# The first SwiGLU block of a decoder trunk: two products advanced together, and the last squares of the final norm summed in PSUM

## The chip, the cores and the metric

The kernel is one program on one core of a Trainium2 chip. The metric is the device time of one execution in microseconds; three executions of the kernel before took 2440.54, 2441.75 and 2447.37 us, median 2441.75 us.

## What the kernel computes

A decoder trunk of two layers over 512 tokens of width 1024, in fp32. Each layer adds four sublayers to the residual stream, each on an RMS-normed input: a SwiGLU feed-forward block (weight 1/2), a token mixer (short convolution, a gated recurrence and an RWKV-7 group side by side), cross-attention into 256 memory tokens, and a second feed-forward block. A final RMSNorm ends it. The parts that the change touches are the first feed-forward block and the two ends of the norm:

```
def rmsnorm(x, g):
    xf = xf * lax.rsqrt(jnp.mean(xf * xf, axis=-1, keepdims=True) + EPS)
    return (xf * g)
def swiglu_ffn(x, w_in, w_out):
    gate, up = jnp.split(x @ w_in, 2, axis=-1)       # 2 x 2816 columns
    return (jax.nn.silu(gate) * up) @ w_out
h = x
for l in range(2):
    h = h + 0.5 * swiglu_ffn(rmsnorm(h, ffn1_norm[l]), ffn1_w_in[l], ffn1_w_out[l])
    ...
return rmsnorm(h, final_norm)
```

## The kernel before

The stream is held transposed: `h[0]` to `h[7]`, each 128 of the 1024 channels by 512 tokens. Every large product runs in a split form: an operand is a high part (rounded to fp32r by ScalarE) and a low part (the rest, by VectorE), and `mm3` issues three matmuls: high x high, high weight x low input, low weight x high input. One product of a 128-column weight block with the eight chunks is 24 matmuls of 128x512 into one PSUM bank. The factor of the norm is not applied to the input: the gain of the norm is folded into the split of `h[d]`, and the product is multiplied by the reciprocal root afterwards (`gated`, with `n.rstd`).

A feed-forward block goes through 22 pairs of weight blocks (f = 0 to 21, in three slabs of 8, 7 and 7): a gate product, an up product, then `gated` on VectorE and ScalarE, which frees the two banks. After each slab eight output products add to `h`. Below, W0 and U0 are the gate and up weights of f = 0, G1 and U1 those of f = 1, G2 the gate weights of f = 2.

`load_w` brings one weight block: a copy issued by SP into a staging buffer (`wst`, two of them), the high part on ScalarE (`whi`, three) and the low part on VectorE (`wlo`, three). `Weights` keeps the planned sequence; `take` hands out the next block and calls `ahead(2)`, and `group` calls `ahead(3)` after a product, so loads are asked for two or three blocks ahead. PSUM's eight banks are three `pb` (`big`), three `pm` (`small`) and two `pt` (`serial`, otherwise used by the mixer).

The order on TensorE is the order of the program. ScalarE and VectorE get an order from a clock model in the kernel: each instruction is given a modelled start, and `issue_in_order` chains the instructions of each of the two engines by it. The order on SP is left to the framework, which lets copies go ahead of where the program asks for them: the four copies of `memT`, asked for at f = 9, are issued at 15.35 us. The mixing stages are also interleaved by a planner (`Fill.run`) that reads the same clock model.

The beginning: `start` loads W0 in four pieces of 256 columns, and behind the copy of each piece it issues two chunks of x and their splits; then come the eight squares (`Norm.chunk`, ScalarE) and seven adds (VectorE) whose column sums give the first norm. `ffn` then runs the gate product of f = 0 into `pb`, the up product (its weights U0 loaded whole), loads the constants `cst`, runs the gate product of f = 1, asks for the sums (`n.begin`: `rms_sums`, 4 fp32 matmuls against ones, then VectorE, GpSimd, VectorE), runs the up product of f = 1 into a `pm` bank, and only then spreads the factor over the partitions (`rms_spread`, 8 small matmuls) for `gated`. The gate product of f = 2 takes the `pb` bank that `gated` of f = 0 frees.

The end: as each of the last eight output products is added to `h[d]`, `chunk(d)` squares it, adds the square to `acc` and scales a copy by the gain. After the last one `rms_sums`, `rms_spread`, eight multiplications and eight copies out follow.

Lines: in the trace all instructions of VectorE, ScalarE and SP carry line 285 and those of TensorE line 340, the two recording helpers, so the tiles tell them apart: `s` is any 128x512 slot, `xT` the input, `pb`, `pm`, `pt` the banks.

Of the kernel before, what the change touches and what calls it, by code (L numbers as in the profile page):

```python
# [11 lines left out]
F32R = mybir.dt.float32r  # L12
I32 = mybir.dt.int32
AF = mybir.ActivationFunctionType
ALU = mybir.AluOpType
# [3 lines left out]
P = 128  # L19
# [310 lines left out]
def trunk(ctx: ExitStack, tc: tile.TileContext, a, out, parts=("ffn1", "mix", "xa", "ffn2"), dbg=None):  # L330
# [38 lines left out]
    def f32(x):  # L369
        return x.bitcast(F32)  # L370
# [53 lines left out]
    def col(l, name, i=0):  # L424
        o = l * VL + VOFF[name] + i
        return vec[:, o:o + 1]
# [31 lines left out]
        ve.tensor_scalar(omka[:, l * 3:l * 3 + 3], vec[:, o:o + 3], -1.0, 1.0, ALU.mult, ALU.add)  # L458


    def load_w(src, cols, piece=1024, between=None):
        st, hi, lo = wst.get(), whi.get(F32R), wlo.get(F32R)
        for o in range(0, cols, piece):
            cs = slice(o, min(cols, o + piece))
            sp.dma_start(st[:, cs], src[:, cs])
            if between:
                between(o // piece)
            se.activation(hi[:, cs], st[:, cs], AF.Copy)
            ve.tensor_tensor(lo[:, cs], st[:, cs], f32(hi[:, cs]), op=ALU.subtract)
        return hi, lo  # L470

    class Weights:
# [138 lines left out]
            ve.scalar_tensor_tensor(lo, src, scale, f32(hi), op0=ALU.mult, op1=ALU.subtract)  # L611
        return hi, lo

    def rms_sums(acc, n):

        k = n // P
        ps = small()
        for i in range(k):
            te.matmul(ps[:, i:i + 1], acc[:, i * P:(i + 1) * P], ones[:, 0:1], start=True, stop=True)
        r = clock.tile(tiny, [P, 4], F32, "rms", 4)  # L620
        ve.tensor_scalar(r[:, :k], ps[:, :k], 1.0 / D, EPS, ALU.mult, ALU.add)
        gp.tensor_tensor(r[:, :k], r[:, :k], mhalf.to_broadcast([P, k]), op=ALU.pow)
        rh = clock.tile(tiny, [P, 4], F32R, "rmsh", 4)
        rl = clock.tile(tiny, [P, 4], F32R, "rmsl", 4)
        ve.tensor_copy(rh[:, :k], r[:, :k])
        ve.tensor_tensor(rl[:, :k], r[:, :k], f32(rh[:, :k]), op=ALU.subtract)
        return rh, rl
# [11 lines left out]
    class Norm:  # L639
        def __init__(self, l, name):  # L640
            self.l, self.name = l, name
            self.acc = self.r = self.sums = self.waiting = None
            self.x = []
            self.scaled = []

        def chunk(self, d):
            if self.acc is None:
                self.acc = sl.get()
                se.activation(self.acc, h[d], AF.Square)
            else:  # L650
                sq = sl.get()
                se.activation(sq, h[d], AF.Square)
                ve.tensor_tensor(self.acc, self.acc, sq, op=ALU.add)
                sl.put(sq)
            if self.name is not None:
                self.x.append(split(h[d], col(self.l, self.name, d)))
            elif self.l is None:
                y = sl.get()
                se.activation(y, h[d], AF.Copy, scale=vec[:, L * VL + d:L * VL + d + 1])
                self.scaled.append(y)  # L660

        def begin(self):
            if self.sums is None:
                self.sums = rms_sums(self.acc, T)
                sl.put(self.acc)

        @property
# [21 lines left out]
                sl.put(*x)  # L689
            sl.put(self.r)  # L690

    def start(name, src):

        n = Norm(0, name)

        def load(i):
            for d in (2 * i, 2 * i + 1):
                sp.dma_start(h[d], a["xT"][:, d, :])
                n.x.append(split(h[d], col(0, name, d)))

        W.plan[0][2] = load_w(src, 1024, 256, load)
        n.name = None
        for d in range(ND):
            n.chunk(d)
        return n


    def ffn(l, which, n, nxt, between=None):
# [13 lines left out]
        for f0, f1 in SLABS:  # L722
            act = []
            for f in range(f0, f1):
                if f in between:
                    between[f]()
                pg = big()
                group(pg, w_in[l, f], 1024, n.x)
                if f or "w" not in between:
                    n.begin()  # L730
                pu = small() if first else big()
                group(pu, w_in[l, NF + f], 1024, n.x)
                if f == 0 and "w" in between:
                    first = pg, pu
                    sp.dma_start(cst, a["cst"])
                    ve.tensor_copy(identr, ident)
                    continue
                if first:
                    gated(*first)
                    first = None  # L740
                gated(pg, pu)
            last = f1 == NF
            if last:
                n.release()
            for d in range(ND):
                po = big()
                k = f1 - f0
                group(po, w_out[l, d, :, f0 * P:f1 * P], k * P, act)
                ve.scalar_tensor_tensor(h[d], po, 0.5, h[d], op0=ALU.mult, op1=ALU.add)
                if last:  # L750
                    nxt.chunk(d)
            for x in act:
                sl.put(*x)
# [866 lines left out]
    plans = {"ffn1": lambda l: plan_ffn(l, 1), "mix": plan_mix, "xa": plan_xa, "ffn2": lambda l: plan_ffn(l, 2)}  # L1620
    for l, s in steps:
        plans[s](l)
    n = start("ffn1_norm", a["ffn1_w_in"][0, 0])
    for i, (l, s) in enumerate(steps):
        nxt = Norm(steps[i + 1][0], norms[steps[i + 1][1]]) if i + 1 < len(steps) else Norm(None, None)
        if s == "ffn1":
# [75 lines left out]
```

## Time and profile before

| | us |
|---|---|
| median of three executions | 2441.75 |
| the profiled execution | 2447.83 |
| its span, first to last instruction | 2446.0 |
| TensorE busy in the span | 2398.0 |
| VectorE busy | 1389.6 |
| ScalarE busy | 995.7 |
| first matmul | 7.66 |
| last large matmul ends | 2429.55 |

Times in the rows are counted from the start of the span. A timeline row gives start, length, engine, line, operation, output <- inputs, and how many instructions are merged in it; in brackets stands the engine's idle time before it and what ended that. Consecutive matmuls overlap in the record, so the pace is read from start to start.

### The profile page before, as it was taken

The page shows a single profiled execution, that of the slowest core. Times are in us where ns is not written, and L with a number is a line of the kernel's source. Part 1 is how long each engine was busy: PE and PEld are TensorE (multiplying, and loading weights), DVE is VectorE, ACT ScalarE, POOL GpSimd, SP SyncE. Part 2 cuts the span into 40 slices and gives each one's busy share as a digit, 9 for nine tenths or more (in the row PEclk, how much of TensorE's full clock was granted, in tenths as well). Part 3 has the DMA queues.
Part 4 walks back from the last instruction along what each step waited for, and adds up shares of the span by engine and source line. Part 5 has one row for each costly group of instructions (what it writes and reads, how often), then busy time and mean ns, then how long its engine had stood idle before and what let it go on. Part 6 is the DMA issues. An engine that isn't in the chain of part 4 may idle for free. (4 is left out here: it accounts for less than half of the span.)

```text
span 2446.0 us, 33922 instructions
## 1 busy us (share of the span) xinstructions
PE 2398.0 (98%) x13812; PEld 1971.5 (81%) x13812; DVE 1389.6 (57%) x2172; ACT 995.7 (41%) x1416; POOL 20.8 (1%) x22
## 2 busy tenths in 40 slices
PE   7999999999999999999999999999999999999997
PEld 6888887787878888888888888877887788888886
DVE  5444456798866654444544444567987756434444
ACT  4222235756654432222332222466475534323222
POOL 0000000000000000000000000000000000000000
PEclk9999999999999999999999999999999999999998
DMA  5333333243422233333323333423333313232332
GB/s 166 95 95 94 99 109 103 82 150 122 134 84 80 65 103 97 102 93 97 95 95 100 98 95 95 132 82 121 121 117 118 96 48 100 92 98 94 96 99 74
DMA packets 94315, 246.84 MB, mean 101 GB/s; under 512 B 22096, under 2 KB 24784, under 8 KB 94160
## 3 DMA queue, kind: packets, MB, share of 16 engines
q1 hardware_dynamic: 90848, 238.56, 31.6%
q10 hardware_dynamic: 3312, 6.12, 0.7%
q8 instruction: 109, 1.79, 0.3%
q14 instruction: 46, 0.38, 0.1%
HBM read 230.48 MB, written 14.16 MB: 100 GB/s over the span
## 5 line engine op out<-in xcount | busy, mean ns | idle before, releaser
L340 PE MATMUL pb<-s,whi 128*128 128x512 f32 (+1 forms) x6160 | 1897.6, 390 | 24.3 <-ACT whi L285 16.7
L340 PEld LDWEIGHTS pb<-s,whi 128*128 128x128 f32 x6160 | 1150.2, 189 | 268.1 <-ACT whi L285 20.6
L340 PE MATMUL pb<-s,wlo 128*128 128x512 f32 (+1 forms) x3080 | 1193.5, 388 | 5.6 <-DVE wlo L285 5.6
L285 ACT ACTIVATE whi<-wst 128x1024 fp32r<-128x1024 f32 (+5 forms) x445 | 434.2, 976 | 1033.9 <-PE pb L340 637.6
L340 PEld LDWEIGHTS pb<-s,wlo 128*128 128x128 f32 x3080 | 582.9, 189 | 123.9 <-DVE wlo L285 7.7
L285 DVE TENSOR_TENSOR wlo<-wst,whi 128x1024 fp32r<-128x1024 f32 (+5 forms) x445 | 498.4, 1121 | 134.8 <-ACT whi L285 127.1
L285 DVE TENSOR_TENSOR s<-pb,s 128x512 f32<-128x512 f32 (+1 forms) x345 | 236.0, 689 | 465.0 <-PE pb L340 443.4
L285 ACT ACTIVATE s<-s 128x512 f32<-128x512 f32 (+2 forms) x458 | 282.7, 626 | 246.8 <-DVE s L285 241.2
L285 DVE TENSOR_TENSOR s<-s,s 128x512 f32<-128x512 f32 (+3 forms) x526 | 317.0, 621 | 97.0 <-ACT s L285 92.1
L285 DVE SCALAR_TENSOR_TENSOR s<-pb,s 128x512 f32<-128x512 f32 x96 | 66.4, 692 | 234.5 <-PE pb L340 234.5
L285 ACT ACT_TABLE_LOAD x74 | 94.9, 1283 | 2.9 <-PEq L1690 1.7
L285 DVE SCALAR_TENSOR_TENSOR s<-s,vec,s 128x512 fp32r<-128x512 f32 (+2 forms) x100 | 74.3, 748 | 3.8 <-ACT s L285 2.9
L340 PEld LDWEIGHTS pm<-s,s 64*64 64x64 f32 (+2 forms) x1104 | 60.4, 158 | 10.0 <-issue 4.3
L340 PE MATMUL pm<-s,s 64*64 64x64 f32 (+2 forms) x1104 | 66.7, 248 | 1.7 <-DVE s L285 0.9
L285 ACT ACTIVATE s<-s,vec 128x512 fp32r<-128x512 f32 (+1 forms) x90 | 64.3, 718 | 3.3 <-DMA s<-xT 1.7
L340 PE MATMUL pb<-whi,s 128*128 128x512 f32 x128 | 49.5, 427 | 3.3 <-DVE s L285 3.3
L340 PEld LDWEIGHTS pm<-s 64*64 64x64 f32 (+1 forms) x1152 | 33.8, 132 | 4.7 <-issue 3.2
L340 PE MATMUL pm<-s 64*64 64x32 f32 (+1 forms) x1152 | 36.3, 216 | 0.0
L285 POOL TENSOR_TENSOR rms<-rms,mhalf 128x4 f32<-128x4 f32 (+1 forms) x10 | 17.1, 1714 | 2120.7 <-DVE rms L285 2120.7
L340 PEld LDWEIGHTS pb<-whi,s 128*128 128x128 f32 x128 | 24.1, 188 | 10.8 <-DVE s L285 4.1
L285 DVE TENSOR_TENSOR s<-s 128x256 f32<-128x256 f32 (+1 forms) x79 | 31.7, 439 | 0.2
L285 ACT ACTIVATE s<-pb 128x512 fp32r<-128x512 f32 x32 | 19.0, 594 | 29.5 <-PE pb L340 29.2
(106 smaller groups left out, 741.1 us busy)
## 6 DMA issues: line engine op xcount, KB each, us to landing
wst<-ffn_w_in SPq DMA_DIRECT2D x175, 512.0 KB, 3.4
wst<-w_mix_in SPq DMA_DIRECT2D x58, 512.0 KB, 3.6
wst<-ffn_w_out SPq DMA_DIRECT2D x64, 448.0 KB, 3.3
wst<-ffn_w_out SPq DMA_DIRECT2D x32, 512.0 KB, 3.5
wst<-xattn_wk SPq DMA_DIRECT2D x16, 512.0 KB, 4.4
wst<-xattn_wv SPq DMA_DIRECT2D x16, 512.0 KB, 3.7
wst<-xattn_wq SPq DMA_DIRECT2D x16, 512.0 KB, 3.5
wst<-xattn_wo SPq DMA_DIRECT2D x32, 256.0 KB, 2.6
```

What stands on the lines that cost most here:

```text
L285: ins = fn(*args, **kw)
L340: self.pin(nc.tensor.matmul(*args, **kw))
```

## The change

`start` now takes the sources of both W0 and U0, and issues for each quarter a piece of W0, a piece of U0 and two chunks of x; the splits follow in the order piece of W0, chunk, piece of U0, chunk. Behind the last chunk it issues the copy of `cst`, `W.ahead(3)` (the load of G1) and the copy of the identity, all ahead of the squares. For f = 0 of the first block `ffn` takes both weights, and advances the two products in turns, three matmuls each per chunk; the banks are one `pb` and one `pt`. The second `take` asks for U1's load before the 48 matmuls. The up product of f = 1 goes to the other `pt`. The call of `n.begin` that asks for the sums stands behind the gate product of f = 1, where it stood. In the final norm the square of the last chunk isn't added to `acc`: `rms_sums` issues four matmuls on `acc` and four more, accumulating, on the last square.

```diff
--- before.py
+++ after.py
@@ -458,15 +458,12 @@
         ve.tensor_scalar(omka[:, l * 3:l * 3 + 3], vec[:, o:o + 3], -1.0, 1.0, ALU.mult, ALU.add)
 
 
-    def load_w(src, cols, piece=1024, between=None):
+    def load_w(src, cols):
         st, hi, lo = wst.get(), whi.get(F32R), wlo.get(F32R)
-        for o in range(0, cols, piece):
-            cs = slice(o, min(cols, o + piece))
-            sp.dma_start(st[:, cs], src[:, cs])
-            if between:
-                between(o // piece)
-            se.activation(hi[:, cs], st[:, cs], AF.Copy)
-            ve.tensor_tensor(lo[:, cs], st[:, cs], f32(hi[:, cs]), op=ALU.subtract)
+        cs = slice(0, cols)
+        sp.dma_start(st[:, cs], src[:, cs])
+        se.activation(hi[:, cs], st[:, cs], AF.Copy)
+        ve.tensor_tensor(lo[:, cs], st[:, cs], f32(hi[:, cs]), op=ALU.subtract)
         return hi, lo
 
     class Weights:
@@ -611,12 +608,16 @@
             ve.scalar_tensor_tensor(lo, src, scale, f32(hi), op0=ALU.mult, op1=ALU.subtract)
         return hi, lo
 
-    def rms_sums(acc, n):
+    def rms_sums(acc, n, last=None):
 
         k = n // P
         ps = small()
         for i in range(k):
-            te.matmul(ps[:, i:i + 1], acc[:, i * P:(i + 1) * P], ones[:, 0:1], start=True, stop=True)
+            te.matmul(ps[:, i:i + 1], acc[:, i * P:(i + 1) * P], ones[:, 0:1], start=last is None or i == 0,
+                      stop=last is None, skip_group_check=last is not None)
+        for i in range(k if last is not None else 0):
+            te.matmul(ps[:, i:i + 1], last[:, i * P:(i + 1) * P], ones[:, 0:1], start=False, stop=True,
+                      skip_group_check=True)
         r = clock.tile(tiny, [P, 4], F32, "rms", 4)
         ve.tensor_scalar(r[:, :k], ps[:, :k], 1.0 / D, EPS, ALU.mult, ALU.add)
         gp.tensor_tensor(r[:, :k], r[:, :k], mhalf.to_broadcast([P, k]), op=ALU.pow)
@@ -639,12 +640,15 @@
     class Norm:
         def __init__(self, l, name):
             self.l, self.name = l, name
-            self.acc = self.r = self.sums = self.waiting = None
+            self.acc = self.last = self.r = self.sums = self.waiting = None
             self.x = []
             self.scaled = []
 
         def chunk(self, d):
-            if self.acc is None:
+            if d == ND - 1 and self.name is None and self.l is None:
+                self.last = sl.get()
+                se.activation(self.last, h[d], AF.Square)
+            elif self.acc is None:
                 self.acc = sl.get()
                 se.activation(self.acc, h[d], AF.Square)
             else:
@@ -661,7 +665,7 @@
 
         def begin(self):
             if self.sums is None:
-                self.sums = rms_sums(self.acc, T)
+                self.sums = rms_sums(self.acc, T, self.last)
                 sl.put(self.acc)
 
         @property
@@ -689,16 +693,28 @@
                 sl.put(*x)
             sl.put(self.r)
 
-    def start(name, src):
+    def start(name, srcs):
 
         n = Norm(0, name)
-
-        def load(i):
+        ws = [(wst.get(), whi.get(F32R), wlo.get(F32R)) for _ in srcs]
+        for i in range(4):
+            cs = slice(256 * i, 256 * i + 256)
+            for (st, hi, lo), src in zip(ws, srcs):
+                sp.dma_start(st[:, cs], src[:, cs])
             for d in (2 * i, 2 * i + 1):
                 sp.dma_start(h[d], a["xT"][:, d, :])
+        for i in range(4):
+            cs = slice(256 * i, 256 * i + 256)
+            for u, (st, hi, lo) in enumerate(ws):
+                se.activation(hi[:, cs], st[:, cs], AF.Copy)
+                ve.tensor_tensor(lo[:, cs], st[:, cs], f32(hi[:, cs]), op=ALU.subtract)
+                d = 2 * i + u
                 n.x.append(split(h[d], col(0, name, d)))
-
-        W.plan[0][2] = load_w(src, 1024, 256, load)
+        for e, w in zip(W.plan, ws):
+            e[2] = w[1:]
+        sp.dma_start(cst, a["cst"])
+        W.ahead(3)
+        ve.tensor_copy(identr, ident)
         n.name = None
         for d in range(ND):
             n.chunk(d)
@@ -724,17 +740,20 @@
             for f in range(f0, f1):
                 if f in between:
                     between[f]()
+                if f == 0 and "w" in between:
+                    first = big(), serial()
+                    two = [group_steps(ps, W.take(w_in[l, i], 1024), n.x) for ps, i in zip(first, (0, NF))]
+                    for _ in zip(*two):
+                        pass
+                    for g in two:
+                        next(g, None)
+                    W.ahead(AHEAD)
+                    continue
                 pg = big()
                 group(pg, w_in[l, f], 1024, n.x)
-                if f or "w" not in between:
-                    n.begin()
-                pu = small() if first else big()
+                n.begin()
+                pu = serial() if first else big()
                 group(pu, w_in[l, NF + f], 1024, n.x)
-                if f == 0 and "w" in between:
-                    first = pg, pu
-                    sp.dma_start(cst, a["cst"])
-                    ve.tensor_copy(identr, ident)
-                    continue
                 if first:
                     gated(*first)
                     first = None
@@ -1620,7 +1639,7 @@
     plans = {"ffn1": lambda l: plan_ffn(l, 1), "mix": plan_mix, "xa": plan_xa, "ffn2": lambda l: plan_ffn(l, 2)}
     for l, s in steps:
         plans[s](l)
-    n = start("ffn1_norm", a["ffn1_w_in"][0, 0])
+    n = start("ffn1_norm", (a["ffn1_w_in"][0, 0], a["ffn1_w_in"][0, NF]))
     for i, (l, s) in enumerate(steps):
         nxt = Norm(steps[i + 1][0], norms[steps[i + 1][1]]) if i + 1 < len(steps) else Norm(None, None)
         if s == "ffn1":
```

## Rows read from the trace of the kernel before

**Rows 1.** The page: busy time by engine, and TensorE's granted clock in 40 slices of the span.
```profile
PE 2398.0 (98%) x13812; PEld 1971.5 (81%) x13812; DVE 1389.6 (57%) x2172; ACT 995.7 (41%) x1416; POOL 20.8 (1%) x22
...
PEclk9999999999999999999999999999999999999998
```
**Rows 2.** Busy time in stretches of the span: stretch, length, busy us (instructions) of TensorE, its weight loads, VectorE, ScalarE, GpSimd; mean granted clock; DMA share; GB/s.
```profile
15.51:20.49 4.98, 0.74 (x4) 0.30 (x3) 4.57 (x7) 3.31 (x5) 0.00 (x0) 0.85 0.84 290
...
33.55:42.89 9.34, 7.40 (x42) 6.27 (x40) 3.52 (x7) 3.97 (x5) 1.93 (x1) 1.00 0.20 58
42.89:46.40 3.51, 3.51 (x8) 2.81 (x9) 3.42 (x6) 2.39 (x4) 0.00 (x0) 0.51 0.51 149
46.40:2429.55 2383.15, 2362.08 (x13677) 1942.52 (x13675) 1357.12 (x2105) 970.95 (x1380) 17.68 (x16) 0.99 0.32 99
2429.55:2446.00 16.45, 3.36 (x16) 3.12 (x16) 6.79 (x13) 1.83 (x3) 1.01 (x1) 0.58 0.34 128
```
**Rows 3.** Timeline of TensorE, first 47 us.
```profile
7.66 1.22 PE L340 MATMUL pb<-s,whi 128*128 128x512 f32 x2 [7.66 <-ACT whi L285]
...
12.38 0.40 PE L340 MATMUL pb<-s,wlo 128*128 128x512 f32 x1
...
15.13 0.39 PE L340 MATMUL pb<-s,wlo 128*128 128x512 f32 x1
17.92 0.73 PE L340 MATMUL pb<-s,whi 128*128 128x512 f32 x2 [2.40 <-ACT whi L285]
20.49 0.80 PE L340 MATMUL pb<-s,wlo 128*128 128x512 f32 x1 [1.84 <-DVE wlo L285]
...
25.78 0.43 PE L340 MATMUL pb<-s,wlo 128*128 128x512 f32 x1
...
33.55 0.95 PE L340 MATMUL pm<-cst,s 128*128 128x1 f32 x8
...
39.94 0.22 PE L340 MATMUL pm<-identr,rmsh 128*128 128x128 f32 x1
...
42.89 1.22 PE L340 MATMUL pb<-s,whi 128*128 128x512 f32 x2 [1.94 <-DVE s L285]
...
46.40 0.39 PE L340 MATMUL pb<-s,wlo 128*128 128x512 f32 x1
```
**Rows 4.** Timeline of ScalarE, first 19 us.
```profile
5.29 0.72 ACT L285 ACTIVATE s<-s,vec 128x512 fp32r<-128x512 f32 x1 [1.17 <-DMA s<-xT]
...
7.21 0.40 ACT L285 ACTIVATE whi<-wst 128x256 fp32r<-128x256 f32 x1
...
11.07 1.38 ACT L285 ACTIVATE s<-s,vec 128x512 fp32r<-128x512 f32 x2
...
12.66 4.26 ACT L285 ACTIVATE s<-s 128x512 f32<-128x512 f32 x8
16.82 1.99 ACT L285 ACTIVATE whi<-wst 128x1024 fp32r<-128x1024 f32 x2
```
**Rows 5.** Timeline of VectorE, 5 to 22 us.
```profile
6.04 0.75 DVE L285 SCALAR_TENSOR_TENSOR s<-s,vec,s 128x512 fp32r<-128x512 f32 x1 [0.44 <-ACT s L285]
...
13.83 5.47 DVE L285 TENSOR_TENSOR s<-s,s 128x512 f32<-128x512 f32 x7 [0.25 <-ACT s L285]
19.22 2.35 DVE L285 TENSOR_TENSOR wlo<-wst,whi 128x1024 fp32r<-128x1024 f32 x2
```
**Rows 6.** The copies: a stretch of 2 us (columns as in rows 2), two kinds of copy of the first 24 us with count, KB each and median us from issue to landing, and two issues on SP.
```profile
8.00:10.00 2.00, 2.00 (x6) 1.41 (x6) 2.00 (x5) 2.00 (x4) 0.00 (x0) 1.00 1.04 385
...
s<-xT SPq DMA_DIRECT2D x8, 256.0 KB, 4.8
...
cst<-cst SPq DMA_DIRECT2D x1, 736.0 KB, 6.5
...
13.61 0.33 SPq L285 DMA_DIRECT2D wst<-ffn_w_in  x1
15.35 2.71 SPq L285 DMA_DIRECT2D s<-memT  x4
```
**Rows 7.** Timeline of VectorE in the steady part of the block: the first read of each product's bank, for two products in a row.
```profile
50.25 0.69 DVE L285 TENSOR_TENSOR s<-pb,s 128x512 f32<-128x512 f32 x1 [3.04 <-PE pb L340]
...
55.69 0.69 DVE L285 TENSOR_TENSOR s<-pb,s 128x512 f32<-128x512 f32 x1 [3.30 <-PE pb L340]
```
**Rows 8.** Timeline of the end.
```profile
2429.16 0.39 PE L340 MATMUL pb<-s,wlo 128*128 128x512 f32 x1
2429.58 0.69 DVE L285 SCALAR_TENSOR_TENSOR s<-pb,s 128x512 f32<-128x512 f32 x1 [2.67 <-PE pb L340]
2430.31 0.63 ACT L285 ACTIVATE s<-s 128x512 f32<-128x512 f32 x1 [3.51 <-DVE s L285]
...
2430.97 0.69 DVE L285 TENSOR_TENSOR s<-s,s 128x512 f32<-128x512 f32 x1 [0.69 <-ACT s L285]
...
2431.72 1.42 PE L340 MATMUL pm<-cst,s 128*128 128x1 f32 x8 [2.17 <-DVE s L285]
2433.18 0.16 DVE L285 TENSOR_SCALAR rms<-pm 128x4 f32<-128x4 f32 x1 [1.51 <-PE pm L340]
```
**Rows 9.** Who waited for whom on TensorE from 45 to 2429 us.
```profile
PE pb L340 <- DVE s L285: 7.9, 6, 2.2
```

## Prediction

> **What bounds the kernel now.** The page comes first: TensorE is busy in 98% of the span, and its granted clock is below full in the last slice alone [rows 1]. So only idle time of TensorE, or time at the lower of its two clocks (1.2 in place of 2.4 GHz), can be won. The stretches then say where that is: from 46.40 to 2429.55 us TensorE idles 2383.15 - 2362.08 = 21.1 us in all; the rest lies in the first 46 us and in the tail [rows 2]. The change touches just these two. So the timeline of TensorE is read there. It starts at 7.66, and stands still three times: 2.40 us before 17.92 (for `whi` of U0), 1.84 before 20.49 (for `wlo` of U0), 1.94 before 42.89 (for a bank that VectorE reads) [rows 3]. The timelines of ScalarE and VectorE show why: ScalarE runs eight squares from 12.66 before the weights at 16.82, VectorE seven adds from 13.83 before `wlo` at 19.22 [rows 4, 5]. At the end every step waits for the last.
>
> The warm pace: a product's 24 matmuls take 55.69 - 50.25 = 5.44 us, 0.227 each [rows 7]. At the lower clock a start comes every 0.43 us: 11 of them from 7.66 to 12.38, 8 from 42.89 to 46.40, 12 from 20.49 to 25.78 [rows 3]; the granted clock of the second of these stretches is 0.51 [rows 2]. So a stall of 1.9 us costs some 1.7 us more behind it.
>
> **The beginning.** Removed are the waits for U0 and for the third `pb` bank; added are three more SP issues, and U0 in four small conversions in place of one large.
>
> First matmul. W0's and U0's first pieces are ahead of chunk 0, so it comes behind 128 KB more. At the 385 GB/s of [rows 6] that is 0.34 us; the queue is not yet at that rate then, so I take 0.6: 5.29 becomes 5.9 [rows 4]. The piece of W0 is now converted ahead of it, not at 7.21 behind chunk 1. With 0.72 us of ScalarE the first matmul is at 6.65; the second needs the low part, 0.75 us of VectorE [rows 4, 5], and starts at 7.4. From both sides: 1.0 us earlier than 7.66, or 0.6 later, if both pieces are converted first.
>
> The 48 matmuls. If the clock rises where it did, about 12.38, then 1 + (12.38 - 7.4) / 0.427 = 12.7 matmuls are out by then. The other 35.3 take 8.0 us at the warm pace: both products end at 20.4. Is x there in time? ScalarE began chunks 6 and 7 at 11.07 and needed both by 11.8 [rows 4]; U0's 512 KB go ahead of the last of them now, 1.36 us at 385 GB/s, so it lands by 13.1. TensorE comes to chunk 7 at 20.4 - 1.4 = 19.0. The conversions are further ahead too: per two chunks ScalarE needs 2 x 0.72 + 2 x 0.40 = 2.2 us, TensorE 12 x 0.227 = 2.7. So what U0's smaller pieces add on ScalarE and VectorE lies beside TensorE. Changing the bank every three matmuls is not in this trace; the nearest rows change it every 24, inside the 5.44 us, so I take nothing; 0.03 us for each of 15 changes, 0.4 in all, is the upper end, and nothing in the rows suggests a gain.
>
> A rule of the Trainium skill speaks against the pieces: DMA: Bandwidth & Descriptors, section Bandwidth, wants copies batched to 1 MiB and more, and its section Anatomy gives a fixed cost of about 2.0 us each. The trace disagrees for copies in flight together: with pieces of 128 and 256 KB it moved 385 GB/s [rows 6]. By the rule taken one copy at a time, the sixteen copies would take over 32 us and this stage would gain nothing; by the row the sum stands. Its weaker form is rival (2), which is worked out from rows.
>
> G1. Its copy is issued once the last piece of W0 is split (some 12.7 us), behind `cst`: 736 and 512 KB behind 13.1 us at 385 GB/s land at 16.4. With about 1.0 us on ScalarE and 1.2 on VectorE (16.82 to 18.81 and 19.22 to 21.57 for two blocks [rows 4, 5]) `wlo` is there at 18.6; behind all seven adds of VectorE, at 20.7. It is wanted at 20.4 + 2 x 0.227 = 20.85. So no stall is summed, and 2 us of slack is all the cover. U1 is asked for before the 48 matmuls, and its high part waits on ScalarE for a `whi` buffer until W0 is read out, about 20. Behind it in ScalarE's queue stand G2's and later parts; U1 is wanted at 26.7. `identr` waits on VectorE for `cst` among the adds, whose sum is wanted at 25.8: covered as well. SP's queue has `memT` (15.35 [rows 6]) where the framework puts it, which is a rival below.
>
> From there: product G1 to 25.85, the sums 34.36 - 33.55 = 0.81, U1's product to 32.1, the spread about 0.95 (39.94 to 40.9 [rows 3]), and f = 2 at 33.05 on the free third `pb` with the clock up. `gated` of f = 0, which ended the 1.94 us, now has a whole product of 5.44 us beside it before its bank is wanted. The sums stay behind G1's product, and cost what they did. Before, f = 2 started at 42.89 and had 8 matmuls out by 46.40, as much as a warm start at 46.40 - 8 x 0.227 = 44.6. The gain is 44.6 - 33.05 = 11.5 us. It was made up of 6.2 us of stalls, some 4.6 us of the slow clock behind them, and the earlier start.
>
> How long the slow clock lasts at the start is one sample. TensorE: Matmul & The Clock Gate in the Trainium skill, section What's actually happening, says that it varies from run to run, 6, 11 or 14 slow matmuls in one kernel; 11 of before agrees with that. By its ends the 12.7 counted here would give 1.3 us more gain or 0.3 less.
>
> **The end.** The add of the last square, 0.70 us from 2430.97, leaves the chain [rows 8]. The four matmuls on `acc` (eight records) go before the last square is ready; four on `last` take their place. Before, TensorE had stood still for 2.17 us and the eight records took 1.43 us (2431.72 to 2433.15); at the warm clock 0.81 [rows 3, 8]. Now TensorE works until about 2430.4 and stands 0.6, so I take 0.81: a gain of 0.70 + 0.62 = 1.3 us; 0.70 if it is slow already. The spread behind takes 2.0 us to the copy, about 1.0 warm; I leave it slow, and 1.0 more gain is that bound.
>
> **The sum.** 11.5 + 1.3 = 12.8 us. The profiled execution took 2447.83 (its span 2446.0 and 1.83 around it), so 2435.0 by its own time. It lies 6.1 us above the median of the runs; what differs between the runs isn't in the parts that are summed, so I take the 12.8 from the median: 2441.75 - 12.8 = 2428.9.
>
> **The rivals.** (1) G1 comes late: SP puts the four `memT` copies, which wait for adds on VectorE, ahead of it. Then `wlo` is ready some 2.7 us later than 20.7, TensorE stands 2.5 us, and 12 slow matmuls follow at 0.2 extra, 2.4: a gain of 12.8 - 4.9 = 7.9, 2433.9. For it: the framework did hoist `memT`, and the cover is 2 us. Against: `memT` went behind the block that was ready at 13.61 [rows 6].
>
> (2) The pieces hold the interleaved products back, so that the clock stays low through all 48: 48 x 0.43 = 20.6 us from 6.65, 27.3 in place of 20.4: a gain of 5.9, 2435.9. For it: twice the matmuls now hang on each chunk's landing, and SP issues more. Against: supply of 2.2 us beside the 5.1 that TensorE needs for two chunks at the slow pace. Copies that came strictly one after the other, at 4.8 us each [rows 6], would be worse, but before twelve of them had landed by 11.8, so that form gets no chance.
>
> (3) Slower than before: the planner of the mixing stages reads the modelled clock, which is shifted by the new beginning, and the banks and slots turn by one. It could interleave those stages otherwise. Each new stall for VectorE costs up to 2.2 us [rows 9] and about 1.7 of slow clock, 3.9; four of them, 15.6, outweigh 12.8, and give 2444.6. For it: all but 21 us of slack in the middle is in its hands. Against: the rest of the first block runs at TensorE's pace for over 500 us, which leaves only a constant shift.
>
> **How the numbers follow.** Forecast 0.73, (1) 0.14, (2) 0.08, (3) 0.05. The predicted time is 2428.9. The range goes from 2424.5 (1.0 us of an earlier warm spread, 1.3 of a shorter slow start, and 2 us of scatter of a median) to 2437.0 (both slower-starting rivals and 1 us of scatter). A measurement of this kernel tells about 0.3%, 7.3 us, from no change: the line is 2434.4. The forecast falls below it nearly always, (1) slightly more often than not, (2) hardly: faster 0.78, the same 0.17, slower 0.05.
>
> **What would show it.** Right: the first large matmul between 6.5 and 7.5 us; 48 matmuls without a gap to about 20.4; no wait for `whi` or `wlo` of G1; f = 2 at about 33 us with no stall before it; the sums at the end done by 2.4 us after the last large matmul in place of 3.6; the middle stretch with 21 us of idle time as before. Wrong: G1's copy behind `memT` on SP, a low granted clock after 13 us, or more idle time in the middle.

## The result, and the profile after

| us | before | after |
|---|---|---|
| median of six executions | 2441.77 | 2429.16 |
| lowest and highest | 2439.38 to 2447.73 | 2427.98 to 2433.67 |
| the profiled execution, its span | 2447.83, 2446.0 | 2430.36, 2428.6 |

The ratio is 0.9946, 95% interval 0.9933 to 0.9959: 10 to 16 us faster. Forecast were 2428.9 and a gain of 12.8; the medians differ by 12.6.

The page of the kernel after, where rows 1 stood before:

```profile
PE 2389.6 (98%) x13820; PEld 1965.3 (81%) x13820; DVE 1389.5 (57%) x2174; ACT 996.2 (41%) x1419; POOL 19.9 (1%) x22
...
PEclk9999999999999999999999999999999999999998
```

TensorE's busy share is unchanged: 8.4 us of its busy time are gone with the idle time. The stretches of after, cut at the first matmul, where the pace changes, at the end of the first two products, at the gate product of f = 2 and at the last large matmul (columns as in rows 2):

```profile
6.78:12.20 5.42, 5.42 (x12) 3.95 (x13) 5.07 (x10) 4.88 (x11) 0.00 (x0) 1.00 1.07 380
12.20:20.47 8.27, 8.27 (x37) 6.82 (x37) 7.39 (x13) 7.86 (x14) 0.00 (x0) 1.00 0.91 292
20.47:33.15 12.68, 12.68 (x66) 10.74 (x64) 5.66 (x9) 3.35 (x4) 1.01 (x1) 1.00 0.64 208
33.15:2413.11 2379.96, 2359.18 (x13689) 1940.03 (x13688) 1362.86 (x2112) 975.67 (x1386) 17.69 (x16) 1.00 0.32 99
2413.11:2428.60 15.49, 4.07 (x23) 3.74 (x23) 6.09 (x12) 1.83 (x3) 1.01 (x1) 0.57 0.36 135
```

In the first three, length and busy time of TensorE are equal: from its first matmul to f = 2 the record shows no idle time at all, where before it stood 6.2 us. The fourth is the middle: 2379.96 - 2359.18 = 20.8 us of idle time, as before (21.1 in [rows 2]).

TensorE's timeline, the rows that answer to [rows 3]:

```profile
6.78 1.58 PE L340 MATMUL pb<-s,whi 128*128 128x512 f32 x2 [6.78 <-ACT s L285]
...
12.00 0.47 PE L340 MATMUL pt<-s,wlo 128*128 128x512 f32 x1
12.30 0.63 PE L340 MATMUL pb<-s,whi 128*128 128x512 f32 x2
...
20.25 0.39 PE L340 MATMUL pt<-s,wlo 128*128 128x512 f32 x1
20.47 0.62 PE L340 MATMUL pb<-s,whi 128*128 128x512 f32 x2
...
25.91 0.95 PE L340 MATMUL pm<-cst,s 128*128 128x1 f32 x8
...
32.30 0.22 PE L340 MATMUL pm<-identr,rmsh 128*128 128x128 f32 x1
...
33.15 0.67 PE L340 MATMUL pb<-s,whi 128*128 128x512 f32 x2
```

Output `pt` and `pb` alternate; the pace is that of the lower clock to 12.0 and the warm one after; the column of the granted clock has 1.00 there all the same, so at the start the pace is what to read. The product of G1 (`pb` at 20.47) follows the last matmul into `pt` (20.25) at one step's distance, and f = 2 at 33.15 has no bracket: there was no wait. What had to be ready for it, on ScalarE, VectorE and SP:

```profile
6.00 0.72 ACT L285 ACTIVATE s<-s,vec 128x512 fp32r<-128x512 f32 x1 [1.48 <-DMA s<-xT]
...
17.02 1.06 ACT L285 ACTIVATE whi<-wst 128x1024 fp32r<-128x1024 f32 x1 [0.27 <-DMA wst<-ffn_w_in]
```
```profile
12.95 0.42 DVE L285 TENSOR_TENSOR wlo<-wst,whi 128x256 fp32r<-128x256 f32 x1
...
18.11 1.23 DVE L285 TENSOR_TENSOR wlo<-wst,whi 128x1024 fp32r<-128x1024 f32 x1 [0.48 <-ACT whi L285]
```
```profile
9.48 0.43 SPq L285 DMA_DIRECT2D cst<-cst  x1
13.40 1.53 SPq L285 DMA_DIRECT2D wst<-ffn_w_in  x2
16.87 1.13 SPq L285 DMA_DIRECT2D s<-memT  x2
19.37 0.33 SPq L285 DMA_DIRECT2D wst<-ffn_w_in  x1
```

G1's copy and U1's are the two at 13.40, ahead of `memT` at 16.87; G1's goes out when VectorE is done with the last piece of W0 (12.95 + 0.42 = 13.37). G1's high part starts 0.27 us after ScalarE had nothing left, when the copy landed; its low part ends at 18.11 + 1.23 = 19.34. It was wanted by the third matmul of the product, at 20.93: 1.6 us of slack.

The end, where [rows 8] stood:

```profile
2412.71 0.39 PE L340 MATMUL pb<-s,wlo 128*128 128x512 f32 x1
...
2412.94 0.95 PE L340 MATMUL pm<-cst,s 128*128 128x1 f32 x8
...
2413.86 0.63 ACT L285 ACTIVATE s<-s 128x512 f32<-128x512 f32 x1 [3.51 <-DVE s L285]
...
2414.54 1.36 PE L340 MATMUL pm<-cst,s 128*128 128x1 f32 x8 [0.66 <-ACT s L285]
2415.94 0.16 DVE L285 TENSOR_SCALAR rms<-pm 128x4 f32<-128x4 f32 x1 [2.11 <-PE pm L340]
```

The eight records on `acc` come at once behind the last large matmul (2412.94), those on the last square right behind its ScalarE instruction. From the end of the last large matmul to the VectorE instruction behind the sums it is 2.84 us, before 2433.18 - 2429.55 = 3.63.

### The profile page after: what moved, and what is told of

Read it like the earlier page. It is cut to its first block, busy times and chain, and to the rows that moved or that the text cites. A ratio compares the mean times of both kernels' runs of the same rounds, so it can differ in the third digit from the quotient of the medians.

```text
span 2428.6 us, 33949 instructions
## 1 busy us (share of the span) xinstructions
PE 2389.6 (98%) x13820; PEld 1965.3 (81%) x13820; DVE 1389.5 (57%) x2174; ACT 996.2 (41%) x1419; POOL 19.9 (1%) x22
```

## The experiments

Each kernel was timed in five rounds beside the kernel before. The rows of before and after are those of the result, six executions each; the medians of before in the later rounds, 2441.42 to 2441.81, agree with it. The times alone scatter by up to 11.6 us for one and the same kernel (e7), more than most of these parts are worth, so the stages of each profiled execution, one per kernel, are put beside them. "To the sums" is from the first matmul to the sums of the first norm; "middle" is from the first matmul of f = 2 to the end of the last large one, and its idle time; "sums at the end" and "spread" are from the end of the last large matmul to the VectorE instruction behind the sums, and from `rmsh` to the copy of the spread factor.

```
kernel      median   lowest  highest | first  to the  f = 2   middle   idle | sums at  spread
                                     | matmul  sums                         | the end
before      2441.77  2439.38 2447.73 |  7.66   25.89  42.89  2386.66  21.07 |  3.63    2.30
after       2429.16  2427.98 2433.67 |  6.78   19.13  33.15  2379.95  20.79 |  2.84    2.29
e1          2431.72  2430.01 2436.24 |  8.26   18.95  34.44  2379.72  20.69 |  4.07    2.29
e2          2431.89  2430.00 2438.60 |  7.43   19.79  34.45  2379.97  20.80 |  2.54    1.48
e3          2433.26  2432.05 2434.28 |  6.65   19.43  35.42  2381.70  20.80 |  2.54    1.45
e4          2435.47  2433.72 2442.30 |  7.55   19.79  36.68  2381.18  21.00 |  3.26    2.24
e6          2437.56  2430.05 2440.11 |  7.73   20.12  35.09  2379.86  20.75 |  2.53    1.60
e7          2438.39  2430.92 2442.53 |  7.09   20.67  34.99  2379.81  20.72 |  2.54    1.46
e8          2433.93  2429.88 2436.90 |  7.10   17.69  32.02  2387.66  21.34 |  2.79    2.29
e9          2431.50  2428.71 2434.88 |  7.21   19.20  33.64  2383.20  20.84 |  2.67    2.29
e10         2434.91  2429.35 2438.88 |  7.89   19.72  34.85  2386.82  20.72 |  2.53    2.30
e11         2429.93  2428.78 2431.38 |  7.46   19.27  33.96  2379.98  20.72 |  2.53    1.45
e12         2434.47  2432.18 2436.90 |  7.01   18.04  32.28  2382.67  21.32 |  2.53    2.57
```

**e1: the last square added on VectorE again.**

```diff
-            if d == ND - 1 and self.name is None and self.l is None:
-                self.last = sl.get()
-                se.activation(self.last, h[d], AF.Square)
-            elif self.acc is None:
+            if self.acc is None:
```

> The changed kernel with the last square added on VectorE again, so only the beginning is changed. My theory (the tail's part is the 0.70 us add that left the chain, and little of the clock): from the end of the last large matmul to the factor's first VectorE instruction 3.6 us again instead of the 2.83 of the changed kernel, 0.8 us slower than it; beginning unchanged, f = 2 at 33.1 us. Rival (the tail's part is as large as was summed, 1.3 us, or matters to nothing): 1.3 or 0. In time some 11.5 us below the kernel before.

The timeline of its end, VectorE's add and TensorE's sums:

```profile
2415.58 0.69 DVE L285 TENSOR_TENSOR s<-s,s 128x512 f32<-128x512 f32 x1 [0.69 <-ACT s L285]
...
2416.33 1.87 PE L340 MATMUL pm<-cst,s 128*128 128x1 f32 x8 [2.17 <-DVE s L285]
```

The sums take 4.07 us, 1.23 more than after: the 0.69 of the add, and small matmuls of 1.87 in place of 1.36 us. The second part is not the add's: the granted clock in these matmuls was 0.50 here and 0.71 after. To see the add alone, take two kernels that ran them at 1.00, e4 (old end) and e2 (new end), both below; e4 first:

```profile
2420.03 1.05 PE L340 MATMUL pm<-cst,s 128*128 128x1 f32 x8 [2.17 <-DVE s L285]
```
```profile
2415.86 1.05 PE L340 MATMUL pm<-cst,s 128*128 128x1 f32 x8 [0.66 <-ACT s L285]
```

Their sums at the end are done after 3.26 and 2.54 us: the add is worth 0.7. And the matmuls are as fast behind a wait of 2.17 us as behind one of 0.66, so the new end is not what made them fast. The beginning is the same kernel as after, yet chunk 0 landed so that the first matmul came at 8.26: that start moves by 1.6 us between profiled executions (6.65 in e3).

**e2: the two products one after the other.**

```diff
-                    for _ in zip(*two):
-                        pass
-                    for g in two:
-                        next(g, None)
+                    for g in two:
+                        for _ in g:
+                            pass
```

> The changed kernel, with all its loads and splits where they are, but the product with W0 runs to its end before the product with U0 begins. My theory (the gain came from U0's weights being ready ahead of the squares and adds, and not from the turns): the first product waits here and there for x and ends at about 15.7 us, the second at 21.1, against 20.47 for both in turns: 0.6 us slower than the changed kernel, f = 2 at about 33.8. Rival (the turns are what fills TensorE while x arrives): several us of waits and a longer slow clock, 3 us or more slower than the changed kernel, f = 2 at 36 or later.

```profile
7.43 1.58 PE L340 MATMUL pb<-s,whi 128*128 128x512 f32 x2 [7.43 <-ACT s L285]
...
16.31 0.63 PE L340 MATMUL pt<-s,whi 128*128 128x512 f32 x2
...
21.77 0.61 PE L340 MATMUL pb<-s,whi 128*128 128x512 f32 x2
```

The rows are its timeline of TensorE: W0's product, U0's from 16.31, G1's from 21.77. Both take 21.77 - 7.43 = 14.34 us, in turns 20.47 - 6.78 = 13.69: 0.65 us, as expected. No wait stands in brackets in between; the last two chunks of W0's product (14.50 to 16.08) come 0.1 to 0.2 us late at three places. The stage to the sums is 0.66 longer. The turns are not what the gain is made of.

**e3: the old banks.**

```diff
-                    first = big(), serial()
+                    first = big(), big()
-                pu = serial() if first else big()
+                pu = small() if first else big()
```

> The changed kernel with the banks as before: f = 0 in two pb, the up product of f = 1 in a pm, so that f = 2 needs the bank that gated of f = 0 frees. My theory: TensorE stands about 1.9 us before f = 2 and runs some 8 matmuls at the slow clock behind it, 3.6 us slower than the changed kernel. Rival (an earlier beginning leaves VectorE time, so the bank is free): no stall, 0 us.

```profile
35.42 0.73 PE L340 MATMUL pb<-s,whi 128*128 128x512 f32 x2 [1.94 <-DVE s L285]
```

The stall in its timeline is 1.94 us long, to the hundredth that of before [rows 3], and its middle is 1.75 us longer than after's: the slow clock behind the stall. In sum 3.7 us; the medians differ by 4.1. Being 7.5 us earlier (35.42 for 42.89) does not shorten it, because the bank waits for the spread, which TensorE itself runs just before: in e3's trace ScalarE's copy of it starts at 33.51, and VectorE's first read of the bank runs from 34.68 to 35.37.

**e4: only U0's load ahead of the squares.**

```diff
         W.plan[0][2] = load_w(src, 1024, 256, load)
+        W.ahead(2)
```

(on the kernel before)

> The kernel before with one line more: U0's load, in one piece as before, is asked for ahead of the squares and adds. No turns, old banks, old tail. My theory: no stall before U0's product, which follows the first one at about 15.6 us with the clock up; the stall before f = 2 stays. Removed are 2.40 + 1.84 us of stalls and some 2.9 us of slow clock: 7.1 us below the kernel before, about 2434.7. Rival (the pieces and the turns are needed): less than 2 us below before.

```profile
22.22 0.50 PE L340 MATMUL pb<-s,wlo 128*128 128x512 f32 x1 [0.47 <-DVE wlo L285]
...
36.68 1.02 PE L340 MATMUL pb<-s,whi 128*128 128x512 f32 x2 [1.94 <-DVE s L285]
```

Its TensorE timeline has no stall before U0; one of 0.47 us before G1's low part, and the old one before f = 2. To the sums it takes 19.79 us against 25.89: 6.1 us from one line, and 6.3 by the medians (7.1 were expected, of which the new 0.47 us takes a part). The rival, that pieces and turns are needed, falls. U0's copy itself was issued early already, at 7.61 us in the kernel before; what the line moves ahead of the squares and adds is its splits.

**e6: e4's line, the banks of the change, its end.** On the kernel before:

```diff
+        W.ahead(2)
-                pu = small() if first else big()
+                pu = serial() if first or (f == 0 and "w" in between) else big()
```

and the two edits of the change in `rms_sums` and `Norm.chunk`.

> The kernel before with three small edits: U0's load in one piece ahead of the squares, the two pt banks for the up products of f = 0 and 1, and the last squares summed in PSUM. No pieces of U0, no turns. My theory (the parts add up and the turns give nothing): first matmul at 7.6, no stall before U0, at most 0.5 us before G1's low part, none before f = 2, f = 2 at about 34.7; the tail 1.2 us shorter than before; within 1 us of the changed kernel, about 2430. Rival (pieces and turns give several us): 2433 or more.

```profile
22.69 0.50 PE L340 MATMUL pb<-s,wlo 128*128 128x512 f32 x1 [0.59 <-DVE wlo L285]
```

By its stages it is the changed kernel with 1.0 us more to the sums, of which 0.59 is the wait for G1 in the row of its timeline; there is no stall before f = 2 and the sums at the end take 2.53. Its median, 2437.56, says otherwise: the expectation of 2430 failed, and the time lies where the rival put it, though the stages show nothing of the rival's several us. Its twelve executions lie in two clusters, five from 2430.05 to 2431.44 at a granted clock of 0.994 or 0.995, seven from 2436.16 to 2440.11 at 0.990 to 0.992. The profiled one is of the first cluster; that the second differs from it in the middle is an inference from its clock (last section).

**e7: G1's load asked for behind the squares.**

```diff
-        W.ahead(3)
         ve.tensor_copy(identr, ident)
...
             n.chunk(d)
+        W.ahead(3)
```

> The changed kernel with the load of G1 asked for behind the squares, so that ScalarE splits it after eight squares and VectorE after seven adds. My theory: its low part is ready at about 21.4 us, wanted at 20.9: a stall of 0.5 us, too short for the clock to fall, 0.5 us slower than the changed kernel in the beginning. Rival (a late G1 costs a stall with a slow clock behind it): 4 to 5 us slower.

```profile
22.62 0.50 PE L340 MATMUL pb<-s,wlo 128*128 128x512 f32 x1 [0.64 <-DVE wlo L285]
```

A stall of 0.64 us, 0.5 expected, and the pace behind it in its timeline stays at the warm one: no fall of the clock. (The stage is 1.5 us longer in all; the pace also changed later here, at 13.6 against 12.0. The median, 2438.39, is again that of executions between 2430.92 and 2442.53, ten of the twelve at 2436.47 and above; whether the late G1 has a part in that isn't shown.) So losing the slack of G1 in this way costs little in its stage. A wait of 2.5 us, which rival (1) priced with 4.9 us, was not produced.

**e8: TensorE warmed while x is on its way.** Three fp32 matmuls on a zeroed slot ahead of everything:

```diff
+        z = sl.get()
+        gp.memset(z, 0.0)
+        pw = small()
+        for _ in range(3):
+            te.matmul(pw, z[:, 0:P], z, start=True, stop=True)
+        sl.put(z)
         n = Norm(0, name)
```

> The changed kernel with three fp32 matmuls of 128x512 on a zeroed slot ahead of everything, into a pm bank that nobody reads, while TensorE would wait for x. My theory (some 2.3 us of the beginning are the slow clock alone): the clock is up when the first product starts or soon after, both products end some 2 us earlier after the first matmul than in the changed kernel (13.7 us from first matmul to the end of both), then up to 1.2 us of that is given back waiting for G1's low part: 1 to 2.5 us faster than the changed kernel. Rival (matmuls on zeros don't raise the clock, or they hold up the first product): no gain or a loss of about 1 us.

```profile
1.31 4.73 PE L340 MATMUL pm<-s 128*128 128x512 f32 x6 [1.31 <-POOL s L285]
7.10 0.50 PE L340 MATMUL pb<-s,whi 128*128 128x512 f32 x1 [1.06 <-ACT s L285]
7.88 0.50 PE L340 MATMUL pb<-s,whi 128*128 128x512 f32 x1 [0.29 <-DVE s L285]
...
19.66 0.50 PE L340 MATMUL pb<-s,wlo 128*128 128x512 f32 x1 [0.37 <-DVE wlo L285]
```

Its timeline: the added matmuls end at 6.04, the first product runs warm soon after, and the sums come 17.69 us after the first matmul of that product, 1.4 less than after; 0.37 us go to waiting for G1. f = 2 is 1.1 us earlier. But the profiled execution is no faster (2436.90, the slowest of seven; the fastest took 2429.88), since its middle is 7.7 us longer with only 0.55 us more idle time. Two stretches of 6 us, the first with a stall among the output products of the first layer's mixer, the second behind two short waits ahead of its second feed-forward block, after first and e8 second:

```profile
704.00:710.00 6.00, 4.56 (x20) 3.80 (x21) 4.79 (x7) 2.14 (x4) 0.00 (x0) 1.00 0.39 112
857.00:863.00 6.00, 6.00 (x30) 5.02 (x30) 1.69 (x4) 0.68 (x2) 1.91 (x1) 1.00 0.29 87
```
```profile
704.00:710.00 6.00, 5.14 (x16) 4.15 (x17) 3.47 (x6) 1.32 (x3) 0.00 (x0) 0.72 0.42 122
857.00:863.00 6.00, 5.89 (x23) 4.91 (x24) 1.71 (x5) 1.06 (x1) 1.88 (x1) 0.72 0.30 108
```

TensorE stood 2.16 us before 705.44 in the one and 2.13 before 704.86 in the other; the granted clock is 1.00 in the one and 0.72 on the mean in the other. It is the same in the second stretch, ahead of which TensorE had stood 0.50 and 0.28 us in after, 0.53 and 0.28 in e8. So a wait of 0.5 us is not always as harmless as in e7, though which wait brought the lower clock there isn't shown. After has four stretches at the lower clock in its middle, e8 eight.

**e9: lowrank's copy off the front.**

```diff
-        se.dma_start(lr, a["lowrank"][l])
+        sp.dma_start(lr, a["lowrank"][l])
```

> The changed kernel with the copy of lowrank (384 KB, used only by the mixer) issued on SP, where it goes behind U1's load, and not on ScalarE's queue at 1.2 us. My theory (chunk 0 shares the copy engines with lowrank): 384 KB less in front bring chunk 0 about 0.7 to 1.0 us earlier, the first matmul at about 5.9 and with less scatter, and the end of both products 0.2 to 1 us earlier. Rival (the landing of chunk 0 is set by latency and by SP's issues): first matmul at 6.8 as in the changed kernel.

```profile
6.43 0.72 ACT L285 ACTIVATE s<-s,vec 128x512 fp32r<-128x512 f32 x1 [2.00 <-DMA s<-xT]
```

A miss: on ScalarE's timeline chunk 0 is taken up at 6.43, with lowrank ahead of it at 6.00 (after) and 5.88 to 7.49 in the others. No gain of 0.7 to 1.0 us shows; against a scatter of 1.6 us one execution can't exclude a small one. What moves the landing by 1.6 us stays open.

**e10: the first staging buffer held back.**

```diff
+        for _ in range(2):
+            gp.memset(ws[0][0], 0.0)
         for i in range(4):
```

> The changed kernel with two memsets of the first staging buffer on GpSimd ahead of the first copy, which start everything some 1.6 us later and change nothing else. My theory (the middle, from f = 2 to the last large matmul, has the same 20.8 us of idle time in every run, but its length moves by several us with the number of its stalls that find the clock lowered): first matmul at about 8.4, beginning 1.6 us later, the same idle time in the middle, and a time that differs from the changed kernel's by something else than 1.6 us, anywhere from -2 to +8, with a lower granted clock in the slower executions. Rival (what the beginning gains or loses is carried to the end one to one): 1.6 us slower than the changed kernel, 2430.8, with the same scatter.

```profile
0.74 0.38 SPq L285 DMA_DIRECT2D s<-xT  x1
...
2.72 1.28 SPq L285 DMA_DIRECT2D wst<-ffn_w_in  x3
```

The edit did not shift everything alike: on SP only the copy of W0 into that buffer waits for the memsets, until 2.72, and the first two chunks of x go out ahead of it, where in after W0's piece is the first copy, at 0.74.

```profile
21.23 0.73 PE L340 MATMUL pb<-s,whi 128*128 128x512 f32 x2 [0.49 <-ACT whi L285]
22.49 0.50 PE L340 MATMUL pb<-s,wlo 128*128 128x512 f32 x1 [0.53 <-DVE wlo L285]
```

The first matmul came only 1.1 us later than after's, and the later G1 brought two waits of 0.49 and 0.53 us in the rows of its timeline. f = 2 is 1.7 us later than after's. Idle time in the middle is 20.72, yet the middle is 6.9 us longer, and the executions run from 2429.35 at a clock of 0.995 to 2438.88 at 0.990. For the median one to one does not hold: it is 5.7 us up for a beginning that ends 1.7 later. Between the fastest executions, 2429.35 and 2427.98, the difference is 1.4.

**e11: small matmuls to keep the clock up at the end.** Two on the identity between the sums on `acc` and those on the last square, six behind:

```diff
+        if last is not None:
+            hum(2)
...
+        if last is not None:
+            hum(6)
```

> The changed kernel with eight more fp32 matmuls of 128x128 on the identity, into a bank that nobody reads: two between the sums on acc and those on the last square, six behind them. My theory (the tail's small matmuls cost what they do because the clock falls while TensorE waits): the sums of the last square 0.8 to 0.9 us, the spread 1.0 in place of 2.0, the tail 1 to 1.5 us shorter. Rival (the small matmuls are slow by their form, or the added ones are in the way): tail the same or longer.

```profile
2415.38 1.05 PE L340 MATMUL pm<-cst,s 128*128 128x1 f32 x8
2416.29 1.58 PE L614 MATMUL pm<-cst 128*128 128x128 f32 x12
2418.13 0.30 PE L340 MATMUL pm<-identr,rmsh 128*128 128x128 f32 x1 [0.26 <-DVE rmsh L285]
```

Its timeline at the end: the sums take 1.05 us (1.36 after), and from `rmsh` to the copy it is 1.45 in place of 2.29. The tail is 1.1 us shorter, from 15.50 to 14.36 us behind the last large matmul. But this does not show that the added matmuls did it: e2, e3 and e7, which have none, end in the same way (sums 1.05, spread 1.45 to 1.48, tail 14.3 to 14.4), and e12, which has the same eight, has a slow spread. What the runs do show is that these matmuls are slow by the clock and not by their form: the same eight records take 1.05 us at a granted clock of 1.00 (e2, e4), 1.36 at 0.71 (after) and 1.87 at 0.50 (e1). The median, 2429.93, is that of the changed kernel within its scatter: its first matmul came 0.7 us later.

**e12: e8 and e11 together, and seven small matmuls ahead of the last chunk of the first query product of each layer's cross-attention**, which was taken for the place of the stalls of 2.16 us:

```diff
+            if late and k == n - 1:
+                hum(late)
```

> The changed kernel with the warm start and the tail's added matmuls, and seven more of them ahead of the last chunk of the first query product of each cross-attention, where TensorE stands 1.9 to 2.2 us for the last chunk's split. My theory: beginning 1 to 1.5 us and tail 1 to 1.5 us shorter than in the changed kernel, no fall of the clock at the two cross-attentions, about 2426 in the better executions, 2 to 3 us below the changed kernel. Rival (the gain at the front is lost again in the middle by other stalls that find the clock lowered): no faster than the changed kernel.

```profile
704.59 0.70 PE L340 MATMUL pb<-s,whi 128*128 128x512 f32 x2 [2.16 <-DVE s L285]
```
```profile
L616 PE MATMUL pm<-cst 128*128 128x128 f32 x44 | 6.6, 308 | 0.0
```

The place was read wrongly. In its timeline the stall stands where it stood in after, 2.16 us long, among the mixer's output products, where no small matmul had been put; idle time in the middle is 21.32 us, not less. The second row is the group of all small matmuls: 6.6 us, of which 3.2 lie at the end (0.69 and 2.50 in the timeline there) and 3.4 in the middle, where they covered no wait. The middle is 2.7 us longer than after's, the beginning 1.1 shorter to the sums, and no execution is below 2432.18. So it says nothing on whether the clock can be kept up through the stalls; that stays untried. At the end the small matmuls behind the sums took 2.50 us (1.58 in e11) and the spread stayed slow (2.57).

No version ran clearly below the changed kernel.

## Why the prediction was right

**First matmul and the 48.** 6.65 was summed, 6.78 measured; both products end at 20.47 for 20.4. Chunk 0 was taken at 6.00 for 5.9. That the clock would rise where it did held (pace change at 12.0 to 12.3, behind 12 matmuls for the 12.7 counted). In part this is luck. The five other kernels that begin with the same copies (e1, e2, e3, e7, e11) have their first matmul at 6.65 to 8.26 and the change of pace at 12.7 to 13.6, so that the early first matmul is not sure to come again; the kernels with the old start have theirs at 7.55 to 7.73.

**G1.** Its copy was issued at 13.40, not 12.7, since VectorE finished the last piece of W0 only at 13.37, and `wlo` was ready at 19.34, inside the 18.6 to 20.7 of the sum. Rival (1) did not occur: the framework put `memT` behind U1. Its price was not tested: waits of 0.47 to 0.64 us for G1 in e4, e6 and e7 had no slow clock behind them, but the rival's wait was 2.5 us.

**U1, the sums, f = 2.** Sums at 25.91 (25.85), f = 2 at 33.15 (33.05), with no stall: the third `pb` bank did what was said, 3.7 us by e3. The beginning's gain is 44.6 - 33.15 = 11.4 for 11.5.

**Where the text let a reader credit the wrong part.** The working took U0's pieces and the turns as the means to remove the stalls. e2, e4 and e6 show that one line, U0's load ahead of the squares, brings 6.1 of the 11.4 us and the banks 3.7; the earlier first matmul of this execution is worth 0.9; pieces and turns bring 0.7 to 1.0 and most of the risk of supply that rival (2) priced. Rival (2) itself did not occur: the pace was the warm one from 12.3 on, and no wait for a split shows.

**The end.** 1.3 was summed, 0.8 measured at the sums in the profiled pair. The add's 0.70 is right (0.7 between e4 and e2). The 0.62 for warm sums is the term that was wrong, in size and in reason. In size: 0.81 us was read from start to next start and set against 1.43 to the end of the record; to that end the eight records take 1.05 at the full clock, and in after, where the clock fell in the midst of them, 1.36. The sign that was named, sums done by 2.4 us, was missed: 2.84, and 2.53 at best. In reason: the text had the shorter wait of TensorE keep the clock up, but e4 ran them at the full clock behind the old wait of 2.17 us, and after lost it behind one of 0.66. The spread, left slow at no gain, was warm in e2, e3, e6, e7 and e11: 1.45 to 1.60 for 2.29, inside its bound of 1.0.

**The sum and the median.** In the profiled pair the spans differ by 17.4 us, not by 12.8: 11.4 in the beginning, 0.95 in the tail, and 5.0 in the middle, which the change doesn't touch (2386.66 less the 1.70 us of slow clock behind before's last stall, against 2379.95). The 5.0 are accounted for by three stretches at the lower clock: before's middle has seven beside the one behind the removed stall, after's four. So the gain had to be taken from the median and not from the profiled execution, and the reason that the text gave holds in the main, as the table shows: idle time 20.7 to 21.3 in each kernel, lengths from 2379.7 to 2387.7. Not wholly, since the first matmul and the sums at the end, which are summed, scatter too.

That 12.6 came out for 12.8 is in part luck. The stages of the pair are worth 12.4, and the lowest executions of the two kernels differ by 11.4; the medians come near the sum because the middles of the two sets of six executions can then hardly differ on the median. In e6 it is otherwise: its stages gain 9.5 us in the beginning (44.6 - 35.09) and 1.7 in the tail, its median 4.2. So the mechanism is shown by the stages; that the time came out to 0.3 us says less.

**Rival (3)**, a planner that orders the mixer otherwise: the list of waits of TensorE in the middle is nearly the same after as before, where rows 9 stood:

```profile
PE pb L340 <- DVE s L285: 7.9, 6, 2.2
```

It did not occur; of the larger rows only one differs, four waits for low parts, 3.5 us for 3.8. Yet the middle can give back what the front gains by another way that the rivals lacked: the clock.

## What to carry to other kernels

When an engine that bounds a kernel waits at a stage's start, look first at what stands in the queue ahead of the operand it waits for: here one load whose splits were moved ahead of eight squares and seven adds was worth more than the new order of the products. A bank that is freed by a chain through the same engine is a stall of fixed length, and one more bank in the rotation removed it whole here. And a change of a few us should be read from its own stages in the trace, not only from the median, when the rest of the kernel scatters by more.

## What the runs showed of the hardware that was not expected

A stall of the same place and length is followed by the lower clock in one profiled execution and not in another: 2.16 and 2.13 us ahead of 705 us, 1.00 and 0.72 granted in the 6 us around it. The length of the middle goes with the number of such stretches. Six kernels with four of them (after, e1, e2, e6, e7, e11) lie within 0.3 us, from 2379.72 to 2379.98; e9 with six has 2383.20, e10 and e8 with eight 2386.82 and 2387.66: 1.6 to 1.9 us each. (E12 has three, but 3.4 us of added matmuls.) Executions of one kernel follow the mean granted clock over the span: after took 2427.98 to 2428.72 at 0.995 and 2433.67 at 0.992, e10 2429.35 at 0.995 and 2438.88 at 0.990. In the profiled executions of e8 and e10, whose beginnings end 1 or 2 us earlier or later, other stalls were hit than in after; but executions of one program differ as much, so it isn't shown that the shift did it. So a gain at the front can be lost for the most part (e6), or look larger than it is (17.4 for 12.4 in the profiled pair), by stalls that it leaves as they are; what decides in which execution they are hit was not tested.

The landing of the first chunk moves as well: ScalarE takes it up between 5.88 and 7.49 us in six kernels that begin with the same copies (after, e1, e2, e3, e7, e11), and at 6.43 with 384 KB taken out of its way (e9).
